# Splitting attention's queries and keys into rounded part and rest at the projection instead of at each head

## The chip, the cores and the metric

The kernel runs on one core of one Trainium2 chip. The metric is the device time of one execution in microseconds; the time before is the median of three runs. The engines are named as in the profile: PE is TensorE's matrix multiplication and PEld its loading of weights, DVE is VectorE, ACT is ScalarE, POOL is GpSimd, SP is SyncE, which here only issues transfers. ACT and POOL issue transfers too.

## What is computed

One layer of a hybrid encoder, for a prompt of 2048 rows of 1024 and for eight short samples of 16 rows each, with shared weights, all in fp32:

```
h = RMSNorm(x);  z = h @ w_in          # q, k, v of attention; q, k, v, o and gates of an mLSTM
A = chunk-band attention               # 8 heads x 64, chunks of 64, own chunk and 8 before it
B = mLSTM matrix memory                # 4 heads x 128, blocks of 64 in the reference
x = x + RMSNorm(concat(RMSNorm_A(A), sigmoid(o) * headRMSNorm_B(B)) @ w_out)
x = x + RMSNorm(ConvFFN(RMSNorm(x)))   # up, causal depthwise conv, gated GELU, down; D_FF = 2816
```

The outputs are the new x of both groups, the last 512 keys and values of the prompt, the samples' keys and values, and the mLSTM and convolution states.

## The kernel before, in words

Matrix products are done in three passes at fp32r, TensorE's rounded form of fp32: each operand is split into a rounded part (hi) and the rest (lo = value minus hi), and `mm3` (L93 to L97) adds hi x hi, hi x lo and lo x hi. ACT makes hi by a copy into an fp32r tile, DVE makes lo by a subtraction.

**Stage 1, the projection** (`hymba_step`, the loop over `seq`): the prompt's rows are done in two halves, 14 groups of weight columns in each. Groups `qk0` to `qk3` give attention's queries and keys, two heads each, transposed (columns on partitions, rows on the free axis), by `group_T`: six accumulators a group, three for the queries and three for the keys, each of 384 rows (256 for the last of the second half), each of 24 matmuls into one of the two PSUM banks of the tag `mm`. When an accumulator is done, ACT copies it to a tile `qk_st` in SBUF (`evac_scaled`, L224 and L226; the queries are scaled there), and `store_T` (L239) issues the stores to DRAM tensors `qTd`, `kTd` of one pair of heads and 512 rows each, from ACT's queue; the last 512 rows and the samples' rows also go to the outputs. `qk_st` has two buffers.

**Attention** is worked in beside the projection. `load_head` takes a head and a segment of 512 rows. First it fetches the 64 partitions of its queries twice (L334), onto partitions 0 to 63 and 64 to 127 of a raw tile, and those of its one or two segments of keys twice also (L337). Then ACT rounds the queries (L342) and DVE turns the upper half into the rest (L343), and for each segment of keys ACT makes `kh` (L346) and DVE `kl` (L347); values are fetched into raw tiles (L351) and split later (L355, L356). So the queries' two parts lie on the two halves of the partitions, and `att_unit` gets the scores of 128 rows from two matmuls (L382, L383), one with `kh` and one with `kl`, each summing over hi and lo of the queries. Then come bias and minimum on DVE (L393), exp on ACT (L394), PE transposes (`pt`), the split of the weights (L405 on ACT, L406 on DVE) and the product with the values (`ot`, L418, L419). The raw tiles have three buffers, `kh`, `kl` and `qs` two each.

**What sets the order.** `pump` is a planner: the projection yields declared costs (PE, DVE) after every 12 matmuls, and `pump` steps two pipes, attention and mLSTM, in turn while the declared DVE time is below `SHARE` times the declared PE time, at most two steps a call. `load_head` declares 0.6 + 0.6 for each segment of keys for its splits. Afterwards the framework orders each engine's instructions, and the issues of transfers, by its own estimate of when they become ready; on the chip each queue runs in that order.

**Stage 2**, `project`: the product with w_out, 17 tiles of 128 rows, with what is left of attention and the mLSTM worked in until tile 8. For tiles 0 to 7 the turned rows pass through the `mm` banks, which the product uses too, for later ones through the `big` banks (L67, L198, L199). **Stage 3** is the feed-forward part, more than half of the span, in three blocks of rows.

The samples' keys are split in `keys` inside `attention_sample`, in the same `kh` and `kl` tiles; this work stays.

Of the kernel before, what the change touches and what calls it, by code (L numbers as in the profile page):

```python
# [10 lines left out]
F32 = mybir.dt.float32  # L11
F32R = mybir.dt.float32r
# [5 lines left out]
P = 128  # L18
# [26 lines left out]
def hymba_step(ctx: ExitStack, tc: tile.TileContext, I: dict, O: dict):  # L45
# [14 lines left out]
    def ps_sm(name):  # L60
        return psum.tile([P, 512], F32, tag="sm", name=name)

    def dt_(shape, name):
        return dram.tile(shape, F32, tag=name, name=name)

    def transpose(out, in_, n=P):
        nc.tensor.transpose(out, in_, ident[:n, :n])  # L67
# [31 lines left out]

    kTs = dt_([P, 4, 128], "kTs")  # L100
    vs = dt_([P, 512], "vs")
    kTd = [[dt_([P, 512], f"kTd{p}_{s}") for s in range(4)] + [kTs[:, p, :]] for p in range(4)]
    qTd = [[dt_([P, 512 if s < 4 else 128], f"qTd{p}_{s}") for s in range(5)] for p in range(4)]
    vd = [[dt_([P, 4, 256], f"vd{p}_{s}") for s in range(4)] + [vs[:, p * 256:(p + 1) * 256].unsqueeze(1)]
          for p in range(2)]
    qkbd = [[dt_([P, 2, 512 if s < 4 else 128], f"qkbd{p}_{s}") for s in range(5)] for p in range(4)]
# [56 lines left out]
        return iter([])  # L163

    EARLY = 2
    SHARE = 0.615
    clock = [0.0, 0.0]
    turn = [0]
    pipes = []
# [69 lines left out]
                nc.scalar.dma_start(d[:, off:off + n * P], stage[:, j * P:(j + n) * P])  # L239
            j += n  # L240

    def group_T(wh, wl, half, chunks, dsts, scales, name, outs=(None, None)):
        for c in range(2):
            for ci, tiles in enumerate(HALVES[half]):
                n = len(tiles) * P
                ch = chunks[ci]
                acc = ps_mm(f"{name}_{c}_{ci}")
                for k in range(KT):
                    w = slice(k * 256 + c * P, k * 256 + (c + 1) * P)
                    mm3(acc[:, :n], wh[:, w], wl[:, w], ch[:, 0, k, :n], ch[:, 1, k, :n],  # L250
                        start=(k == 0), stop=(k == KT - 1))
                    if k % 4 == 3:
                        yield n * 12 / 2400, 0.0
                stage = pa.tile([P, 384], F32, tag="st", name=f"{name}_st{c}_{ci}", bufs=2)
                evac_scaled(stage[:, :n], acc[:, :n], scales[c])
                store_T(stage, dsts[c], tiles, outs[c])
# [64 lines left out]
    def load_head(s):  # L321
        pair, kg, hh, h, nm = s.pair, s.kg, s.hh, s.h, s.nm
        if kg % 2 == 0:
            nb = pa.tile([P, 640], F32, tag="nb", name=f"nb{nm}", bufs=2)
            nc.sync.dma_start(nb, bias_src(h, P, 640))
            nc.gpsimd.memset(nb[0:64, 576:640], BIG)
            nc.gpsimd.memset(nb[64:128, 0:64], BIG)
            nbs[hh] = nb
        s.nb = nbs[hh]
        rows = slice(hh * 64, hh * 64 + 64)  # L330
        qr = raw_tile(f"qraw{nm}")[:, :512]
        krs = [raw_tile(f"kraw{nm}_{g}")[:, :512] for g in s.segs]
        for r in range(2):
            nc.sync.dma_start(qr[r * 64:r * 64 + 64, :], qTd[pair][kg][rows, :])  # L334
        for kr, g in zip(krs, s.segs):
            for r in range(2):
                nc.sync.dma_start(kr[r * 64:r * 64 + 64, :], kTd[pair][g][rows, :])  # L337
        yield 0.0, 0.0
        s.kh = pa.tile([P, 1024], F32R, tag="kh", name=f"kh{nm}", bufs=2)
        s.kl = pa.tile([P, 1024], F32R, tag="kl", name=f"kl{nm}", bufs=2)  # L340
        s.qs = pa.tile([P, 512], F32R, tag="qs", name=f"qs{nm}", bufs=2)
        nc.scalar.copy(s.qs, qr)  # L342
        nc.vector.tensor_tensor(s.qs[64:128], qr[64:128], s.qs[64:128], op=ALU.subtract)  # L343
        for si, kr in enumerate(krs):
            c = slice(si * 512, (si + 1) * 512)
            nc.scalar.copy(s.kh[:, c], kr)  # L346
            nc.vector.tensor_tensor(s.kl[:, c], kr, s.kh[:, c], op=ALU.subtract)  # L347
        new = [g for g in s.segs if g == kg or (h, g) not in vhl]
        vrs = [raw_tile(f"vraw{nm}_{g}")[:, :4 * DA].rearrange("p (a d) -> p a d", a=4) for g in new]
        for vr, g in zip(vrs, new):  # L350
            nc.sync.dma_start(vr, vd[h // 4][g][:, :, (h % 4) * DA:(h % 4 + 1) * DA])  # L351
        yield 0.0, 0.6 + 0.6 * len(krs)
        for vr, g in zip(vrs, new):
            t = pa.tile([P, 4, P], F32R, tag="vhl", name=f"vhl{nm}_{g}", bufs=4)
            nc.scalar.copy(t[:, :, 0:DA], vr)  # L355
            nc.vector.tensor_tensor(t[:, :, DA:P], vr, t[:, :, 0:DA], op=ALU.subtract)  # L356
            vhl[h, g] = t
        s.v = {g: vhl[h, g] for g in s.segs}
        if kg % 2:
            for g in s.segs:  # L360
                vhl.pop((h, g))
        yield 0.0, 0.34 * len(new)
# [456 lines left out]
    def attention_sample(b0, b1):  # L819
# [22 lines left out]
        def keys(b, p_):  # L842
            if p_ == 0 and (b % 4 == 0 or b == b0):
                s.own = pa.tile([P, 4, 64], F32, tag="sh", name=f"own{b}", bufs=1)
                nc.sync.dma_start(s.own, kTs[:, :, b // 4 * 64:b // 4 * 64 + 64])
            kr = raw_tile(f"skr{b}_{p_}")
            nc.sync.dma_start(kr[:, 0:512], I["cache_k"][b, p_])
            nc.gpsimd.tensor_copy(kr[:, 512:LS], s.own[:, p_, b % 4 * DS:b % 4 * DS + DS])
            yield 0.0, 0.0
            kh = pa.tile([P, 1024], F32R, tag="kh", name=f"skh{b}_{p_}", bufs=2)[:, :LS]  # L850
            kl = pa.tile([P, 1024], F32R, tag="kl", name=f"skl{b}_{p_}", bufs=2)[:, :LS]
# [349 lines left out]
    for n_, (half, gi) in enumerate(seq):  # L1201
# [10 lines left out]
                            [O["v_prompt"][i], O["v_sample"][i].unsqueeze(1)])  # L1212
        elif g[:2] == "qk":
            it = group_T(wh, wl, half, chunks, [qTd[i], kTd[i]], [-(DA ** -0.5), None], nm,
                         [None, [O["k_prompt"][i], O["k_sample"][i]]])
# [479 lines left out]
```

## Time and profile before

| what | value |
|---|---|
| median of 3 runs | 2788.76 us (2788.08 to 2790.21) |
| profiled execution, first to last instruction | 2784.7 us |
| instructions | 47088 |
| bytes moved by DMA | 486.05 MB, 175 GB/s in the mean |
| mean granted clock of TensorE | 0.998 |

The profile is of one execution. Its span, 2784.7 us, lies 4.06 us under the median of the runs; a time worked out from the span is carried over to the runs by adding these 4.06 us, since the profiled execution's own time from end to end is not among the numbers. A row of the view by windows gives, for a stretch of time, its length, each engine's busy time with the number of its instructions, the granted clock, and the DMA engines' share and rate. A row of waits gives the engine and line that waited, who released it, the sum in us, the number of waits and the longest. A row of a timeline gives start, duration (us), engine, line, operation, and in brackets how long the engine had been idle and who ended it.

### The profile page before, as it was taken

To read this page: it belongs to the slowest core of one execution; us is meant where nothing else is said; L and a number is where in the kernel's file an instruction comes from. 1 tells how busy PE (TensorE), PEld (TensorE's weight loads), DVE (VectorE), ACT (ScalarE), POOL (GpSimd) and SP (SyncE) were. 2 spreads that over 40 slices of the span, in tenths; PEclk is the share of its full clock that TensorE was granted. 3 is DMA by queue.
4 is the path that set the end of the run, shared out by engine and by line. 5 is a ranking of instruction groups with operands and counts; after the bars stand their busy time and mean duration, and the time that the engine had idled before them with its cause. 6 is when DMAs were issued, how large, how long until landed. Compare 5 with 4: busy or idle time off the path is not lost.

```text
span 2784.7 us, 47088 instructions
## 1 busy us (share of the span) xinstructions
PE 2723.8 (98%) x16587; PEld 2548.3 (92%) x16587; DVE 1876.3 (67%) x3447; ACT 1409.1 (51%) x2836; POOL 437.4 (16%) x895
## 2 busy tenths in 40 slices
PE   8999999999999999999999999999999999999998
PEld 7899999998899998888999988899999878999887
DVE  5344455656556668666999986457877864888855
ACT  4355555644356666544454555345455543555543
POOL 1000010212000003244111110011111310222220
PEclk9999999999999999999999999999999999999999
DMA  5544355557555555356655455644544774555585
GB/s 185 155 119 136 103 174 162 164 157 217 162 173 148 144 179 171 107 176 227 187 172 167 167 176 174 219 142 153 160 152 141 276 263 152 172 179 180 192 309 190
DMA packets 311883, 486.05 MB, mean 175 GB/s; under 512 B 55426, under 2 KB 150622, under 8 KB 311518
## 3 DMA queue, kind: packets, MB, share of 16 engines
q1 hardware_dynamic: 271134, 442.92, 50.1%
q10 hardware_dynamic: 38592, 33.83, 3.6%
q0 software_dynamic: 1920, 6.29, 0.6%
q8 instruction: 130, 2.13, 0.3%
q14 instruction: 107, 0.88, 0.1%
HBM read 359.36 MB, written 126.70 MB: 175 GB/s over the span
## 4 chain that ended last, share of the span: by engine, by line
PE 55%; DVE 2%; DMA 1%; issue 1%; ACT 1%; POOL 1%; SPq 0%; DVEq 0%; POOLq 0%; ACTq 0%
PE uec L95 6%; PE uec L96 6%; PE uec L97 6%; PE dn L97 4%; PE dn L96 4%; PE dn L95 4%; PE ua L97 3%; PE ua L95 3%; PE ua L96 3%; PE dnm L97 2%; PE dnm L95 2%; PE dnm L96 2%; PE wo L97 2%; PE wo L95 2%; PE wo L96 2%; PE ub L96 1%
## 5 line engine op out<-in xcount | busy, mean ns | idle before, releaser
L95 PE MATMUL uec<-B,wuh 128*128 128x384 f32 (+1 forms) x720 | 234.9, 328 | 2.2 <-DVE uu L1419 1.1
L96 PE MATMUL uec<-B,wuh 128*128 128x384 f32 (+1 forms) x720 | 235.1, 327 | 0.0
L97 PE MATMUL uec<-B,wul 128*128 128x384 f32 (+1 forms) x720 | 233.9, 327 | 0.0
L1266 DVE TENSOR_TENSOR gl<-gr,gh 128x768 fp32r<-128x768 f32 (+3 forms) x141 | 120.4, 863 | 145.8 <-ACT gh L1265 144.5
L1265 ACT CAST gh<-gr 128x768 fp32r<-128x768 f32 (+3 forms) x141 | 102.0, 735 | 200.1 <-PE dn L96 183.2
L1265 ACT CAST wuh<-wu 128x512 fp32r<-128x512 f32 x255 | 141.7, 617 | 112.1 <-PE uec L96 103.2
L95 PE MATMUL dn<-wdh,gh 128*128 128x512 f32 x466 | 182.4, 391 | 2.3 <-DVE ug L1419 2.3
L96 PE MATMUL dn<-wdl,gh 128*128 128x512 f32 x466 | 183.4, 394 | 0.0
L97 PE MATMUL dn<-wdh,gl 128*128 128x512 f32 x466 | 167.9, 396 | 0.0
L1266 DVE TENSOR_TENSOR wul<-wu,wuh 128x512 fp32r<-128x512 f32 x255 | 164.6, 683 | 2.8 <-DMA x2d<-mx 2.8
L393 DVE CUSTOM_DVE_ANT_0 tmp<-s,nb 128x640 f32<-128x640 f32 (+4 forms) x128 | 94.4, 737 | 96.6 <-PE s L383 94.8
L95 PE MATMUL vo<-wi_h,hT 128*128 128x256 f32 x544 | 155.1, 285 | 0.6 <-DVE mt L199 0.6
L97 PE MATMUL vo<-wi_h,hT 128*128 128x256 f32 x544 | 155.6, 286 | 0.0
L96 PE MATMUL vo<-wi_l,hT 128*128 128x256 f32 x544 | 154.8, 285 | 0.0
L95 PEld LDWEIGHTS uec<-B,wuh 128*128 128x128 f32 x720 | 135.0, 188 | 4.2 <-DVE uu L1419 1.6
L95 PE MATMUL qk<-hT,wi_h 128*128 128x384 f32 (+1 forms) x384 | 128.7, 335 | 7.4 <-ACT qk_st L224 6.6
L96 PEld LDWEIGHTS uec<-B,wuh 128*128 128x128 f32 x720 | 135.2, 188 | 0.2
L97 PEld LDWEIGHTS uec<-B,wul 128*128 128x128 f32 x720 | 135.1, 188 | 0.0
L406 DVE TENSOR_TENSOR ptl<-pt,pth 128x640 fp32r<-128x640 f32 (+4 forms) x128 | 93.6, 737 | 57.1 <-ACT pth L405 56.0
L394 ACT ACTIVATE tmp<-tmp,mn 128x640 f32<-128x640 f32 (+4 forms) x128 | 97.6, 762 | 64.6 <-DVE mn L393 61.9
L96 PE MATMUL qb<-hT,wi_h 128*128 128x384 f32 (+1 forms) x384 | 127.8, 333 | 0.0
L96 PE MATMUL qk<-hT,wi_h 128*128 128x384 f32 (+1 forms) x384 | 127.6, 332 | 0.0
(412 smaller groups left out, 8873.0 us busy)
## 6 DMA issues: line engine op xcount, KB each, us to landing
wu<-in_w_up SPq DMA_DIRECT2D x220, 256.0 KB, 4.1
wu<-wsd SPq DMA_DIRECT2D x176, 256.0 KB, 4.2
wdr<-in_w_down SPq DMA_DIRECT2D x132, 256.0 KB, 5.6
gr<-gd SPq DMA_DIRECT2D x78, 384.0 KB, 3.6
wi_raw<-in_w_in SPq DMA_DIRECT2D x52, 512.0 KB, 4.0
wsd<-ws SPq DMA_DIRECT2D x88, 256.0 KB, 2.8
gd<-g SPq DMA_DIRECT2D x44, 384.0 KB, 3.5
kraw<-kTd SPq DMA_DIRECT2D x112, 128.0 KB, 3.2
```

What stands on the lines that cost most here:

```text
L95: nc.tensor.matmul(out, ah, bh, start=start, stop=False, skip_group_check=onto)
L96: nc.tensor.matmul(out, ah, bl, start=False, stop=False, skip_group_check=onto)
L97: nc.tensor.matmul(out, al, bh, start=False, stop=stop, skip_group_check=onto)
L393: nc.vector.tensor_tensor_reduce(o_, s_, b_, 1.0, 3e38, ALU.add, ALU.min, accum_out=mn)
L394: nc.scalar.activation(tmp[:, :n], tmp[:, :n], AF.Exp, bias=mn, scale=-1.0, accum_out=rsum[:, i % 4, hh:hh + 1])
L406: nc.vector.tensor_tensor(s.ptl[:, sl, qc], ptv, s.pth[:, sl, qc], op=ALU.subtract)
L1265: nc.scalar.copy(h, r)
L1266: nc.vector.tensor_tensor(l, r, h, op=ALU.subtract)
```

## The change

The split moves from the head to the projection. `group_T` gets a flag `parts`, set for the qk groups. With it, a new helper `store_parts` writes hi and lo side by side into one tile of two parts (`sthl`, three buffers), hi by ACT and lo by DVE, both straight from PSUM, and stores both with one transfer to `qTd`, `kTd`, which have now room for both parts. Where the accumulator holds rows that also go to an output (or are a sample's), it is first copied to a tile of SBUF as before, and hi and lo are made from there. `load_head` then fetches the queries' hi onto the lower and lo onto the upper half of the partitions, and both parts of the keys twice, straight into the tiles that PE reads. Its casts and subtractions go. `kh` and `kl` become one tile `khl` of the same size with two buffers. The planner gets other numbers: 0.28 of DVE for every 12 matmuls of a qk group, nothing for `load_head`'s second part, and `SHARE` 0.59 for 0.615. The reserve in SBUF for descriptors of POOL's transfers is set to 4096 bytes per partition.

```diff
-    SHARE = 0.615
+    SHARE = 0.59
...
+    def store_parts(acc, scale, dst, tiles, out, name):
+
+        n = len([t for t in tiles if t != SAMPLE]) * P
+        hl = pa.tile([P, 2, 384], F32R, tag="sthl", name=f"{name}_hl", bufs=3)
+        hi, lo = hl[:, 0, :n], hl[:, 1, :n]
+        src = acc[:, :n]
+        tail = [] if out is None else [t for t in tiles if 12 <= t < SAMPLE]
+        if SAMPLE in tiles or tail:
+            stage = pa.tile([P, 384], F32, tag="st", name=f"{name}_st", bufs=2)
+            evac_scaled(stage[:, :len(tiles) * P], acc[:, :len(tiles) * P], scale)
...
+            src, scale = stage[:, :n], None
+        evac_scaled(hi, src, scale)
+        if scale is None:
+            nc.vector.tensor_tensor(lo, src, hi, op=ALU.subtract)
+        else:
+            nc.vector.scalar_tensor_tensor(lo, src, scale, hi, op0=ALU.mult, op1=ALU.subtract)
+        j = 0
+        while j * P < n:
+            t = tiles[j]
+            m = min(4 - t % 4, n // P - j)
+            nc.scalar.dma_start(dst[t // 4][:, :, t % 4 * P:(t % 4 + m) * P], hl.bitcast(F32)[:, :, j * P:(j + m) * P])
+            j += m
...
                     if k % 4 == 3:
-                        yield n * 12 / 2400, 0.0
+                        yield n * 12 / 2400, 0.28 if parts else 0.0
+                if parts:
+                    store_parts(acc, scales[c], dsts[c], tiles, outs[c], f"{name}_{c}_{ci}")
+                    continue
...
-        qr = raw_tile(f"qraw{nm}")[:, :512]
-        krs = [raw_tile(f"kraw{nm}_{g}")[:, :512] for g in s.segs]
+        khl = pa.tile([P, 2, 1024], F32R, tag="khl", name=f"khl{nm}", bufs=2)
+        s.kh, s.kl = khl[:, 0, :], khl[:, 1, :]
+        s.qs = pa.tile([P, 512], F32R, tag="qs", name=f"qs{nm}", bufs=2)
         for r in range(2):
-            nc.sync.dma_start(qr[r * 64:r * 64 + 64, :], qTd[pair][kg][rows, :])
-        for kr, g in zip(krs, s.segs):
-            for r in range(2):
-                nc.sync.dma_start(kr[r * 64:r * 64 + 64, :], kTd[pair][g][rows, :])
+            at = slice(r * 64, r * 64 + 64)
+            nc.sync.dma_start(s.qs.bitcast(F32)[at, :], qTd[pair][kg][rows, r, :])
+            for si, g in enumerate(s.segs):
+                nc.sync.dma_start(khl.bitcast(F32)[at, :, si * 512:(si + 1) * 512], kTd[pair][g][rows, :, :])
         yield 0.0, 0.0
-        nc.scalar.copy(s.qs, qr)
-        nc.vector.tensor_tensor(s.qs[64:128], qr[64:128], s.qs[64:128], op=ALU.subtract)
-        for si, kr in enumerate(krs):
-            c = slice(si * 512, (si + 1) * 512)
-            nc.scalar.copy(s.kh[:, c], kr)
-            nc.vector.tensor_tensor(s.kl[:, c], kr, s.kh[:, c], op=ALU.subtract)
...
-        yield 0.0, 0.6 + 0.6 * len(krs)
+        yield 0.0, 0.0
...
-    nc = bacc.Bacc("TRN2", target_bir_lowering=False, num_devices=1)
+    nc = bacc.Bacc("TRN2", target_bir_lowering=False, num_devices=1, dynamic_dma_scratch_size=4096)
```

More of the change, by code (lines that the diff above doesn't have):

```diff
@@ L61, in ps_sm, with dt_ @@
         return psum.tile([P, 512], F32, tag="sm", name=name)
-    def dt_(shape, name):
-        return dram.tile(shape, F32, tag=name, name=name)
+    def dt_(shape, name, dtype=F32):
+        return dram.tile(shape, dtype, tag=name, name=name)
     def transpose(out, in_, n=P):
@@ L101, in hymba_step @@
     vs = dt_([P, 512], "vs")
-    kTd = [[dt_([P, 512], f"kTd{p}_{s}") for s in range(4)] + [kTs[:, p, :]] for p in range(4)]
-    qTd = [[dt_([P, 512 if s < 4 else 128], f"qTd{p}_{s}") for s in range(5)] for p in range(4)]
+    kTd = [[dt_([P, 2, 512], f"kTd{p}_{s}") for s in range(4)] + [kTs[:, p, :]] for p in range(4)]
+    qTd = [[dt_([P, 2, 512], f"qTd{p}_{s}") for s in range(4)] + [dt_([P, 128], f"qTd{p}_4")] for p in range(4)]
     vd = [[dt_([P, 4, 256], f"vd{p}_{s}") for s in range(4)] + [vs[:, p * 256:(p + 1) * 256].unsqueeze(1)]
@@ L240, in store_T, with group_T @@
             j += n
-    def group_T(wh, wl, half, chunks, dsts, scales, name, outs=(None, None)):
+    def store_parts(acc, scale, dst, tiles, out, name):
[7 more added lines that the diff above has]
+            evac_scaled(stage[:, :len(tiles) * P], acc[:, :len(tiles) * P], scale)
+            for j, t in enumerate(tiles):
+                c = slice(j * P, (j + 1) * P)
+                if t == SAMPLE:
+                    for d in [dst[4]] + ([] if out is None else [out[1]]):
+                        nc.scalar.dma_start(d, stage[:, c])
+            if tail:
+                m = len(tail) * P
+                nc.scalar.dma_start(out[0][:, tail[0] % 4 * P:tail[0] % 4 * P + m], stage[:, n - m:n])
+            src, scale = stage[:, :n], None
[10 more added lines that the diff above has]
+            j += m
+    def group_T(wh, wl, half, chunks, dsts, scales, name, outs=(None, None), parts=False):
         for c in range(2):
@@ L849, in keys @@
             yield 0.0, 0.0
-            kh = pa.tile([P, 1024], F32R, tag="kh", name=f"skh{b}_{p_}", bufs=2)[:, :LS]
-            kl = pa.tile([P, 1024], F32R, tag="kl", name=f"skl{b}_{p_}", bufs=2)[:, :LS]
+            khl = pa.tile([P, 2, 1024], F32R, tag="khl", name=f"skhl{b}_{p_}", bufs=2)
+            kh, kl = khl[:, 0, :LS], khl[:, 1, :LS]
             nc.scalar.copy(kh, kr)
@@ L1214, in hymba_step @@
             it = group_T(wh, wl, half, chunks, [qTd[i], kTd[i]], [-(DA ** -0.5), None], nm,
-                         [None, [O["k_prompt"][i], O["k_sample"][i]]])
+                         [None, [O["k_prompt"][i], O["k_sample"][i]]], True)
         elif g[:2] == "qb":
```

3 lines of the change are left out of this document (removed).

## The prediction

> **What bounds the kernel now.** I read the page first, then the view by windows cut at the stages, then the waits of PE, then the timeline at the longest of them.
>
> ```profile
> span 2784.7 us, 47088 instructions
> ...
> PE 2723.8 (98%) x16587; PEld 2548.3 (92%) x16587; DVE 1876.3 (67%) x3447; ACT 1409.1 (51%) x2836; POOL 437.4 (16%) x895
> ```
>
> ```profile
> core 0: us, PE busy (x) PEld busy (x) DVE busy (x) ACT busy (x) POOL busy (x), PEclk, DMA share, GB/s
> 48.00:115.00 67.00, 59.58 (x337) 56.84 (x338) 21.75 (x84) 17.24 (x42) 1.35 (x6) 0.97 0.56 160
> 115.00:557.00 442.00, 438.49 (x3218) 431.89 (x3218) 234.09 (x538) 235.70 (x557) 32.54 (x94) 1.00 0.47 143
> 557.00:736.00 179.00, 170.53 (x1140) 159.05 (x1140) 99.52 (x307) 75.66 (x203) 31.11 (x96) 1.00 0.58 177
> 736.00:1045.00 309.00, 305.50 (x2330) 300.85 (x2331) 187.84 (x427) 187.79 (x448) 19.89 (x60) 1.00 0.55 164
> 1045.00:1200.00 155.00, 151.65 (x884) 130.43 (x883) 114.55 (x224) 86.02 (x220) 45.90 (x68) 1.00 0.43 135
> 1200.00:1310.00 110.00, 108.36 (x522) 87.86 (x522) 75.66 (x73) 45.64 (x95) 52.50 (x65) 1.00 0.59 199
> 1310.00:2785.00 1475.00, 1454.64 (x7900) 1347.88 (x7898) 1114.52 (x1751) 734.27 (x1230) 244.08 (x475) 1.00 0.57 188
> ```
>
> PE bounds it: 2784.7 - 2723.8 = 60.9 us idle in all. The change takes no matmul away and adds none, so it can only win idle time of PE, or lose more of it. Idle time in the stages that it touches is length minus busy: 7.4 (the first two qk groups), 3.5, 8.5 (the second half's qk groups), 3.5, 3.4 and 1.6 us, 27.9 together. The feed-forward part, with 20.4 us, runs the same instructions before and after. So nothing above about 28 us can be won, whatever ACT and DVE save. What PE waits for in the first stages:
>
> ```profile
> PE qk L95 <- ACT qk_st L224: 6.6, 2, 3.3
> PE cus L781 <- DMA cs<-in_state_c: 5.0, 6, 2.0
> PE pt L67 <- DVE ptl L406: 1.8, 1, 1.8
> ```
>
> The largest row is two waits for the eviction of a qk accumulator, both before 115 us. The timelines of ACT, PE and PEld there:
>
> ```profile
> 81.98 0.62 ACT L342 CAST qs<-qraw 128x512 fp32r<-128x512 f32 x1 [10.99 <-DMA qraw<-qTd]
> 82.50 0.47 ACT L224 COPY qk_st<-qk 128x384 f32<-128x384 f32 x1
> ...
> 108.02 0.48 ACT L224 COPY qk_st<-qk 128x384 f32<-128x384 f32 x1 [7.30 <-DMA qTd<-qk_st]
> ...
> 83.03 0.45 PE L95 MATMUL qk<-hT,wi_h 128*128 128x384 f32 x1 [3.24 <-ACT qk_st L224]
> ...
> 104.70 0.33 PE L96 MATMUL qk<-hT,wi_h 128*128 128x384 f32 x1
> 104.87 0.34 PE L97 MATMUL qk<-hT,wi_l 128*128 128x384 f32 x1
> 108.55 0.69 PE L95 MATMUL qk<-hT,wi_h 128*128 128x384 f32 x1 [3.34 <-ACT qk_st L224]
> ...
> 108.72 0.33 PEld L96 LDWEIGHTS qk<-hT,wi_h 128*128 128x128 f32 x1
> ...
> 111.60 0.33 PEld L96 LDWEIGHTS qk<-hT,wi_h 128*128 128x128 f32 x1
> 111.92 0.20 PEld L97 LDWEIGHTS qk<-hT,wi_l 128*128 128x128 f32 x1
> ```
>
> In the first, ACT stood 10.99 us at a head's query cast, whose transfer had not landed; the finished accumulator's eviction was queued behind it, PE had no bank and stood 3.24 us. In the second, ACT stood 7.30 us because both `qk_st` buffers still waited for their stores, and PE stood 3.34 us. After that PE ran slow: weight loads start 0.32 us apart from 108.72 to 111.92 (ten steps), where matmuls of the same shape started 0.17 apart before (104.70, 104.87). That is 10 x 0.15 = 1.5 us more, and the granted clock of that window is 0.97.
>
> The Trainium skill, "TensorE: Matmul & The Clock Gate", in "What's actually happening", says that an idle window of about 3.4 us halves TensorE's clock and that the window runs free of the program. The trace agrees so far: of two gaps of nearly one length only one was followed by slow matmuls, for about 3.2 us. By that rule a stall of this length costs up to half as much again, and removing it wins that too; by the waits alone the sum below would lose its term of 1.5.
>
> **The change part by part.**
>
> Casts and subtractions of the heads go:
>
> ```profile
> L342 ACT CAST qs<-qraw x32: 606/617/640, 82.0 to 1118.9; 128x512 fp32r<-128x512 f32 x32
> L343 DVE TENSOR_TENSOR qs<-qraw,qs x32: 689/690/777, 82.6 to 1120.5; 64x512 fp32r<-64x512 f32 x32
> ...
> L346 ACT CAST kh<-kraw x56: 605/620/642, 88.2 to 1118.4; 128x512 fp32r<-128x512 f32 x56
> L347 DVE TENSOR_TENSOR kl<-kraw,kh x56: 678/685/889, 88.8 to 1119.7; 128x512 fp32r<-128x512 f32 x56
> ...
> L226 ACT ACTIVATE qk_st<-qk x24: 378/486/497, 55.7 to 730.6; 128x384 f32<-128x384 f32 x20, 128x256 f32<-128x256 f32 x4
> L224 ACT COPY qk_st<-qk x24: 360/472/480, 70.5 to 747.9; 128x384 f32<-128x384 f32 x20, 128x256 f32<-128x256 f32 x4
> ```
>
> ACT loses 32 x 0.617 + 56 x 0.620 = 54.5 us, DVE 32 x 0.690 + 56 x 0.685 = 60.4. ACT keeps 48 evictions (now hi) and gains 16 casts from SBUF for the accumulators with samples or kept keys; between a 0.36 and a 0.62 row I take 0.45, 7 us. DVE gains 48 subtractions, 40 of them of 384 columns or fewer out of PSUM. The nearest row is a PSUM subtraction's twin, an addition of that shape:
>
> ```profile
> L1493 DVE TENSOR_TENSOR x<-x,uec 128x384 f32<-128x384 f32 x44 | 24.2, 549 | 11.3 <-PE uec L97 11.2
> ```
>
> 48 x 0.549 = 26.4 us. Net: ACT -47, DVE -34 us. Beside a PE that is busy 98% this is worth nothing by itself: cost 0, with the matmuls as cover. What counts is where the two stood in PE's way.
>
> **Stall 1 goes**: ACT no longer waits for a query transfer ahead of an eviction. **Stall 2 goes**: stores now have three buffers, so an eviction waits for the third store back; accumulators come 24 x 0.17 = 4.1 us apart, so a store has 12 us where it had 8, and the wait was 7.3 us with about 3.3 too late. With the slow matmuls: 3.24 + 3.34 + 1.5 = 8.1 us won, at least 0 (if another wait on ACT takes their place, as that of the value split L355, which stays).
>
> **A new wait on banks**: a bank is free only after ACT's hi and DVE's lo, 0.49 + 0.55 = 1.04 us instead of 0.49, plus whatever holds DVE. The other bank's accumulator takes 4.1 us, so 3.1 us of lateness on DVE are free. Queued behind are the stores (on ACT, which now stands until lo is made) and, behind them on ACT, exps and casts of attention and of the next weights. DVE's waits:
>
> ```profile
> DVE tmp L393 <- PE s L383: 94.8, 52, 13.2
> ```
>
> Mean 1.8 us, so the typical one fits. The cost lies between 0 and both stalls over again; in the first groups, where the two evictions above ran late, less is free, so I take 1.0 us, nearest to the mean wait less what ACT's own lateness gives back.
>
> **Transfers.** As many issues as before on SP (64 + 112) and on ACT, but keys move both parts:
>
> ```profile
> kraw<-kTd SPq DMA_DIRECT2D x112, 128.0 KB, 3.2
> ...
> mqk<-qkbd SPq DMA_DIRECT2D x32, 256.0 KB, 3.4
> ...
> svr<-in_cache_v SPq DMA_DIRECT2D x32, 256.0 KB, 4.5
> ```
>
> That is 112 x 128 KB = 14.7 MB more fetched and 2 x 2048 x 512 x 4 B = 8.4 MB more stored, 5% of 486 MB, in a stage whose DMA share is about 0.5. A load takes 3.4 to 4.5 instead of 3.2 us and is asked for one whole head ahead: cost 0, covered by four attention units. The loads now wait on SP for PE to finish the scores of the head two before (`khl`, `qs` have two buffers); queued behind are weight and mLSTM loads. In return the value loads lose their wait for `kl` (a raw buffer):
>
> ```profile
> SPq L351 <- DVE kl L347: 49.4, 16, 8.5
> ```
>
> Bounds: -5.0 (the state loads of the `cus` row, which queue behind them; counted below) to +5.0 (as much again); 0, since no wait of PE above names the loads that queue there now. POOL's smaller reserve touches 24 transfers of the last blocks, issued by an engine 16% busy: 0, or some us if a full reserve holds the small copies behind them.
>
> **The planner.** In a qk group 12 matmuls of 384 declare 1.92, which allowed 0.615 x 1.92 = 1.18 of other work and now allow 0.59 x 1.92 - 0.28 = 0.85, 28% less. So the mLSTM sample batches (`cus`), which wait for their state in those groups, come slower: of their 5.0 us I take 1.5 (0 to 5.0). Elsewhere a head of two segments declares about 8.5 before (1.8 + 0.34 for loads, 4 x 1.33 for scores, 1.0 for outputs) and 6.7 after, so attention runs (8.5 / 6.7) x (0.59 / 0.615) = 1.2 times as fast. Twenty score units come after 1045 us now (the view of the tile `s` from there on):
>
> ```profile
> L393 DVE CUSTOM_DVE_ANT_0 tmp<-s,nb x20: 806/816/825, 1045.9 to 1176.4; 128x640 f32<-128x640 f32 x20
> ```
>
> Forty-four of the second half's 64 units come before 1045, so 1.2 times as many leave about ten or fewer. They are moved to 736 to 1045 us, where PE idled 3.5 of 309 us. What they leave is w_out with less cover: tiles 1 to 7 turn their rows through the banks of the product. Uncovered, each would cost PE (rows of the chain and of the lines) an eviction (DVE copy), the square and cast on ACT and the subtraction, less the transposes:
>
> ```profile
> 1163.83 0.73 ACT mt L1016 x2
> ...
> L1014 DVE COPY mx<-wo x34: 676/681/694, 1056.7 to 1314.6; 128x512 f32<-128x512 f32 x34
> ...
> L198 ACT CAST mt<-mT_pt x25: 564/592/1018, 1039.8 to 1299.9; 128x512 fp32r<-128x512 f32 x16, 128x1024 fp32r<-128x1024 f32 x9
> ```
>
> 0.68 + 0.73 + 0.59 + 0.69 (as L347) - 0.9 = 1.8 us, 12.6 for seven tiles. Against it stand up to 3.4 us of idle time there that attention's own chain makes (L406 above). The later tiles, almost without attention, idle 1.6 in 110 us, no worse: I take 0, between -3.4 and +12.6.
>
> **Sum**: -8.1 + 1.0 - 1.5 + 0 = -8.6 on the span, 2776.1; plus the 4.06 between span and median, 2780.2 us.
>
> **The rivals.**
>
> 1. *The time stays.* ACT and DVE lose work that PE never waited for, and another wait on ACT (L355 for its values, the stores for lo) holds the same two evictions. For it: the value transfers held ACT in the same stretch; 60.9 idle us are mostly elsewhere. Against: the longest wait on ACT, 10.99 us, is removed outright. Time 2788, at most 5 us off.
>
> 2. *Slower: DVE gives the banks back late.* Place: the 48 evictions. It decides where DVE starts lo over 3.1 us after hi. DVE waits up to 13.2 us for scores that PE does in between; if two evictions in each half meet such a wait, four stalls of 3.3 + 0.75 stand where two stood: +8.1, 2797. Against: in the second half's qk groups DVE is busy 56% and attention's scores are absent.
>
> 3. *It gains more*: the `cus` waits (5.0) and attention's chain in w_out (3.4) go as well: -8.1 - 5.0 - 3.4 = -16.5, 2772. For it: both are late chains that slower pumping loosens.
>
> That the split saves nothing and the planner's numbers alone do the work is the part of 3 that a run with the old numbers would tell apart.
>
> **How the numbers follow.** The forecast, 2775 to 2783, has 0.47; rival 3 0.09; rival 1 0.26; rival 2 0.18. A measurement tells 0.2%, 5.6 us, from no change. Faster by more (under 2783.2): 0.47 + 0.09 = 0.56; within: 0.26; slower (over 2794.3): 0.18. Most of the chance, 0.82, lies with faster and no change; the likeliest case alone has 2775 to 2783. The range takes in rival 3 and the uncovered w_out tiles on top of the forecast (2780.2 + 12.6 = 2793): 2769 to 2793, leaving out most of rival 2.
>
> **What would show it.** Right: no wait of PE for a qk eviction near 80 or 105 us, PEclk 1.00 there; 48 new DVE subtractions of about 0.55; `s` hardly after 1060 us; the span from 1310 to the end unchanged. Wrong: rows of PE waiting for DVE's lo or for `khl`; w_out idle over 5 us; a feed-forward part longer than 1475 us, which I have no mechanism for beyond POOL's reserve.

## The result, and the profile after

The changed kernel takes 2837.01 us (median of 4 runs, 2833.34 to 2838.84); the kernel before, run beside it on the same chip, takes 2789.35 us. The ratio is 1.0168 with a 95% interval of 1.0154 to 1.0182: **slower by 1.7%**, where 2780.2 was forecast. The profiled execution has a span of 2837.1 us, 52.4 more than before. These are the rows of its page that answer to those of before:

```profile
span 2837.1 us, 46877 instructions
...
PE 2743.7 (97%) x16587; PEld 2563.4 (90%) x16587; DVE 1840.7 (65%) x3407; ACT 1372.2 (48%) x2764; POOL 432.5 (15%) x895
```

PE does the same 16587 matmuls. It is idle 93.4 us instead of 60.9 (+32.5) and busy 19.9 us longer, which makes the 52.4. The longer busy time is slow matmuls: the mean granted clock fell from 0.998 to 0.991, and 0.9% of 2837 us less 0.2% of 2785 us is the same 20 us. ACT and DVE did get their relief, 36.9 and 35.6 us, and it bought nothing.

Where the time went is read best from the view by windows, cut at the same points of the program: the end of the second query-key group, of the `qb2` group of the first half, of the last query-key group, the first matmul of w_out, the first of the feed-forward part, and the end. Columns are length, then busy time of PE, PEld, DVE, ACT and POOL, PEclk, DMA share and GB/s. First the kernel before:

```profile
0.00:114.50 114.50, 94.16 (x597) 89.89 (x598) 49.94 (x128) 43.50 (x84) 11.34 (x39) 0.99 0.58 177
114.50:401.50 287.00, 287.00 (x2050) 284.02 (x2049) 138.74 (x308) 147.61 (x341) 8.62 (x29) 1.00 0.43 128
401.50:746.60 345.10, 331.59 (x2376) 316.03 (x2375) 200.19 (x551) 169.18 (x432) 55.84 (x162) 1.00 0.58 174
746.60:1045.80 299.20, 297.23 (x2276) 293.05 (x2274) 183.53 (x416) 183.67 (x440) 19.07 (x58) 1.00 0.54 162
1045.80:1313.50 267.70, 262.71 (x1414) 220.30 (x1413) 191.36 (x300) 130.86 (x312) 99.01 (x133) 1.00 0.50 164
1313.50:2784.70 1471.20, 1451.14 (x7885) 1345.07 (x7883) 1112.57 (x1748) 734.27 (x1230) 243.47 (x474) 1.00 0.57 188
```

And the kernel after, cut at the same six points:

```profile
0.00:112.10 112.10, 94.86 (x600) 90.73 (x601) 53.87 (x139) 44.70 (x88) 12.41 (x40) 0.98 0.64 203
112.10:402.70 290.60, 289.70 (x2070) 286.43 (x2069) 130.00 (x302) 136.60 (x325) 6.62 (x29) 1.00 0.56 156
402.70:765.70 363.00, 335.70 (x2337) 320.41 (x2336) 196.94 (x542) 162.92 (x415) 53.03 (x162) 0.97 0.58 173
765.70:1072.40 306.70, 297.63 (x2248) 291.50 (x2247) 153.76 (x360) 160.66 (x382) 14.91 (x51) 0.99 0.65 175
1072.40:1368.10 295.70, 274.60 (x1457) 229.57 (x1457) 191.50 (x319) 132.99 (x327) 100.08 (x140) 0.98 0.51 162
1368.10:2837.10 1469.00, 1451.25 (x7885) 1344.75 (x7883) 1114.61 (x1749) 734.29 (x1230) 245.48 (x474) 1.00 0.57 188
```

The stages differ by -2.4, +3.6, +17.9, +7.5, +28.0 and -2.2 us. The first query-key groups won, as meant. The loss lies after 400 us, most of it in w_out, whose own instructions nobody edited. Length less PE busy is the idle time: of the 34.8 us of new idle time before the feed-forward part, 13.8 lie in the third stage, 7.1 in the fourth and 16.1 in w_out (-3.1 and +0.9 in the first two). PE's waits are no single row but many; these five are longer than in before or new:

```profile
PE mT_pt L67 <- DVE mr L1011: 10.7, 5, 5.3
PE cus L807 <- DMA cs<-in_state_c: 9.1, 3, 5.5
PE ma L724 <- DVE num L730: 4.9, 3, 2.5
PE spt L67 <- ACT stmp L906: 4.1, 2, 3.3
PE sot L97 <- DVE spl L917: 4.0, 2, 2.5
```

None of these tiles (w_out's rows, the mLSTM state, the mLSTM and sample attention chains) is touched by the split. The longest wait of the `cus` row, from the timelines of PE and ACT, and the wait of SP for which the state load stood (the view of waits, 540 to 556 us):

```profile
543.58 0.61 PE L807 MATMUL cus<-cs,qz 128*128 128x129 f32 x4
...
553.00 1.20 PE L807 MATMUL cus<-cs,qz 128*128 128x129 f32 x4 [5.48 <-DMA cs<-in_state_c]
...
556.58 0.41 PE L96 MATMUL va<-wi_l,hT 128*128 128x264 f32 x1
556.80 0.32 PE L97 MATMUL va<-wi_h,hT 128*128 128x264 f32 x1
556.96 0.28 PE L95 MATMUL va<-wi_h,hT 128*128 128x264 f32 x1
```

```profile
SPq L795 <- DMA mixd<-num: 5.2, 1, 5.2
```

The load queue stood 5.2 us at the state load (the profile puts it to an mLSTM store), so the transfer landed late and PE stood 5.48 us. Then the clock: the same four matmuls take 1.20 us where they took 0.61, and steps of 0.22 us go back to 0.12 only at 556.96, 4.0 us on. And the longest wait in w_out, ACT ahead of PE:

```profile
1122.67 0.42 ACT L674 ACTIVATE mvo<-mvo 128x256 f32<-128x256 f32 x1 [4.70 <-DMA mvo<-vobd]
1123.11 0.37 ACT L717 ACTIVATE kw<-ms,colsp 128x128 f32<-128x128 f32 x1
1123.38 0.62 ACT L1042 ACTIVATE mt<-mx 128x512 fp32r<-128x512 f32 x1
1123.90 0.19 ACT L1042 ACTIVATION_READ_ACCUMULATOR mt<-mx 128x1 f32 x1
1124.12 0.63 ACT L1009 ACTIVATE mt<-mr 128x512 fp32r<-128x512 f32 x1
```

```profile
1129.72 1.97 PE L67 MATMUL mT_pt<-ident,mr 128*128 128x128 f32 x8 [5.31 <-DVE mr L1011]
```

ACT stood 4.70 us for an mLSTM value transfer (L674). Behind it in ACT's queue stood the square of w_out's next row (L1009); POOL's root, DVE's scaling and PE's transposes followed from it, and PE stood 5.31 us. In both cases the wait starts with the place that an instruction has in an in-order queue. In the second, the scaling's own 2.56 us (L1011, last section) are nearly half of it, a cost that before has too.

### The profile page after: what moved, and what is told of

Same layout as the page of the kernel before. It is cut to its first block, busy times and chain, and to the rows that moved or that the text cites. A ratio compares the mean times of both kernels' runs of the same rounds, so it can differ in the third digit from the quotient of the medians.

```text
span 2837.1 us, 46877 instructions
## 1 busy us (share of the span) xinstructions
PE 2743.7 (97%) x16587; PEld 2563.4 (90%) x16587; DVE 1840.7 (65%) x3407; ACT 1372.2 (48%) x2764; POOL 432.5 (15%) x895
## 4 chain that ended last, share of the span: by engine, by line
PE 51%; DVE 2%; DMA 1%; issue 1%; ACT 0%; POOL 0%; SPq 0%; DVEq 0%; POOLq 0%; ACTq 0%
PE uec L95 6%; PE uec L96 6%; PE uec L97 6%; PE dn L97 4%; PE dn L96 4%; PE dn L95 4%; PE ua L97 3%; PE ua L96 3%; PE ua L95 3%; PE dnm L97 2%; PE dnm L95 2%; PE dnm L96 2%; PE ub L96 1%; PE ub L97 1%; PE ub L95 1%; PE wo L95 1%
## 5 line engine op out<-in xcount | busy, mean ns | idle before, releaser
L97 PE MATMUL qk<-hT,wi_l 128*128 128x384 f32 (+1 forms) x384 | 129.0, 336 | 0.0
```

The source lines that it names most:

```text
L97: nc.tensor.matmul(out, al, bh, start=False, stop=stop, skip_group_check=onto)
```

## The experiments

Times of kernels sent together are compared with runs of the kernel before on the same chip, which gave medians of 2791 to 2795 us. "Before" and "after" are the two kernels of this case.

### Which part of the edit: reserve, planner's numbers, bytes

**e1**, only the reserve, in before:

```diff
-    nc = bacc.Bacc("TRN2", target_bir_lowering=False, num_devices=1)
+    nc = bacc.Bacc("TRN2", target_bir_lowering=False, num_devices=1, dynamic_dma_scratch_size=4096)
```

> The kernel before with one edit, the descriptor reserve set to 4096 as in the kernel after. If the reserve makes the loss, about 2837 us. By all the other theories (planner numbers, doubled key transfers, new order) the reserve does nothing: 2783 to 2795 us.

Measured 2793.58 us, ratio 1.0001 (0.9991 to 1.0010). The reserve costs nothing.

**e2**, only the planner's numbers, in before:

```diff
-    SHARE = 0.615
+    SHARE = 0.59
-                        yield n * 12 / 2400, 0.0
+                        yield n * 12 / 2400, 0.28 if name[:2] == "qk" else 0.0
-        yield 0.0, 0.6 + 0.6 * len(krs)
+        yield 0.0, 0.0
```

> The kernel before with the changed kernel's three planner numbers (share 0.59, 0.28 reserved in each step of the qk groups, 0 declared for a head's loads) and nothing else. If the planner's numbers make the loss, 2825 to 2845 us. If the doubled key transfers make it, 2775 to 2795 us, since none are doubled here. If any new order of the work would cost as much, something between 2800 and 2850 us, with the loss in other places than in the kernel after.

Measured 2836.8 us, ratio 1.0157 (1.0140 to 1.0174). Three numbers, without one instruction of the split, make a loss of the same size as the whole change.

**e3**, the reverse: after with the planner's numbers of before.

```diff
-    SHARE = 0.59
+    SHARE = 0.615
-                        yield n * 12 / 2400, 0.28 if parts else 0.0
+                        yield n * 12 / 2400, 0.0
-        yield 0.0, 0.0
+        yield 0.0, 0.6 + 0.6 * len(s.segs)
```

> The changed kernel with the three planner numbers of the kernel before (share 0.615, no reserve in the qk groups, 0.6 + 0.6 for each segment of a head). If the planner's numbers make the loss, about 2780 us (the old order with the two eviction stalls gone). If the transfers make it, about 2837 us as after. A time between says how much each has.

Measured 2825.7 us, ratio 1.0112 (1.0093 to 1.0131). The split without the numbers loses too. So neither edit is "the" cause: each alone costs 1.1 to 1.6%, both together 1.7%. Costs that don't add up speak for something that either edit sets off.

**e4**, after with as few key bytes as before:

```diff
-        s.kh, s.kl = khl[:, 0, :], khl[:, 1, :]
+        s.kh, s.kl = khl[:, 0, :], khl[:, 0, :]
-                nc.sync.dma_start(khl.bitcast(F32)[at, :, si * 512:(si + 1) * 512], kTd[pair][g][rows, :, :])
+                nc.sync.dma_start(khl.bitcast(F32)[at, 0, si * 512:(si + 1) * 512], kTd[pair][g][rows, 0, :])
```

> The changed kernel, but a head fetches only the keys' rounded part and uses it in place of the rest too, so that the key loads move 14.7 MB less, as many bytes as before; it leaves out the product with the keys' rest. Order, stores and planner are as after. If the doubled key loads make the loss, 2785 to 2800 us. If the planner's numbers or the order make it, 2830 to 2840 us.

Measured 2838.06 us, ratio 1.0158 (1.0136 to 1.0180). The doubled keys are not it. (The order is nearly but not wholly that of after: 94% of TensorE's steps agree, counted as in the next section.)

### The order held

What both edits share is that the framework orders the instructions anew. Matched in the traces (a step is an operation with its tiles and shape, equal neighbours taken as one), TensorE's order in after agrees with that in before in 67% of the steps, that of e2 in 68%, of e3 in 70%. In e1 it is the same step for step. The re-ordering can be switched off:

```diff
-    with tile.TileContext(nc, schedule_with_timeline_sim=True) as tc:
+    with tile.TileContext(nc, schedule_with_timeline_sim=False) as tc:
```

**e5** is before with that edit, **e6** is e3 with it, **e7** is after with it.

> The kernel before with the framework's own re-ordering switched off (the time simulation of its scheduler), so that each engine takes its work much as the program lists it. It is the base for the next two, which have it off as well. If the re-ordering places the work well, this is slower than before, 2790 to 2850 us; no theory rests on its own value.

> The changed kernel with the planner numbers of before and the re-ordering off: TensorE's order is that of the run e5 but for 15 places in 10955 runs of equal steps, so what is left between the two is the split itself with its stores, loads and waits. If the split costs time (waits of the loads for the scores two heads back, stores behind lo, doubled keys), 20 to 40 us more than e5. If the order made the loss, 0 to 10 us less than e5, as the sum of the prediction had it (8.6).

> The changed kernel with its own planner numbers and the re-ordering off. If the planner's numbers are bad whatever the re-ordering, 20 to 50 us more than e6. If it is only the luck of the order that the re-ordering finds, within 10 us of e6.

Measured: e5 2883.51 us (2881.98 to 2884.69; ratio to before 1.0333), e6 2878.41 (2874.73 to 2879.14; 1.0312), e7 2883.77 (2879.64 to 2886.72; 1.0329). TensorE's steps in e5 and e6 agree in 99.8%. With the order so held the split saves 5 us, in the range that was expected of it, and the 33 us that it lost in e3 are not there. The planner's numbers then cost 5 us (e7 against e6), not 30.

e7 also tells what became of a step of the prediction, that attention runs faster under the new numbers. Each instruction of DVE line 419 (393 in before) is one score unit; what comes after the first w_out matmul is counted (x) in these rows of e6, e7 and after:

```profile
L419 DVE CUSTOM_DVE_ANT_0 tmp<-s,nb x18: 810/816/825, 1084.7 to 1231.4; 128x640 f32<-128x640 f32 x18
```

```profile
L419 DVE CUSTOM_DVE_ANT_0 tmp<-s,nb x3: 814/815/816, 1109.9 to 1118.4; 128x640 f32<-128x640 f32 x3
```

```profile
L419 DVE CUSTOM_DVE_ANT_0 tmp<-s,nb x20: 807/819/826, 1072.7 to 1203.4; 128x640 f32<-128x640 f32 x20
```

As listed, the new numbers leave 3 units instead of 18. As re-ordered, after leaves 20, as many as before left. What the planner lists is not what runs.

**e15** and **e16** repeat e5 and e6 with the share at 0.605 (between the two, TensorE's orders differ in 8 places):

```diff
-    SHARE = 0.615
+    SHARE = 0.605
```

> The kernel before with the re-ordering off and the share at 0.605: the base of the next run in a second order. If the order alone moves the time, another 10 us or more away from the run e5 (2883.5).

> The changed kernel with the planner numbers of before but the share at 0.605 and the re-ordering off; TensorE's order agrees with the run e15 but for 8 places. If the split by itself saves what the prediction said, 3 to 10 us less than e15. If the split itself costs time, 10 to 30 us more.

Measured 2889.8 us (2881.67 to 2894.72; 1.0343) and 2894.59 (2891.28 to 2895.29; 1.0355). Both expectations miss: the base moved 6 us and not 10, and the split costs 5 us here where it saved 5. The saving of the first pair is clear of the spread of its runs; the cost of the second is not, since e15 alone spreads over 13 us. In both a cost of 30 us is excluded. The saving of 8.6 us is excluded by the second pair only, and both pairs stand on an order that is 3% slower than that of before, so what the split is worth in before's own order was not measured.

### Other orders of the old code and of the new

If a new draw of the order costs, it must cost without any part of the change. **e8** and **e9** nudge before's share (0.605 and 0.63; counted as above, TensorE's order agrees in 89% and 92% of the steps), **e10** and **e11** do the same to e3, **e12** sets after's share to 0.61. All of them are the edit

```diff
-    SHARE = 0.615
+    SHARE = 0.605
```

with the values named (e12 goes from 0.59 to 0.61).

> The kernel before with its share nudged from 0.615 to 0.605 and nothing else; TensorE's order agrees with that of before in 92% of its steps. If the time hangs on the exact order (before stands on a tuned point), 10 to 40 us more than before. If only the larger moves of the changed kernel's numbers cost, within 6 us of before.

> The kernel before with its share at 0.63 in place of 0.615 (TensorE's order agrees in 91% of its steps). If before stands on a tuned point of the order, a nudge to this side costs as the one to 0.605 did: 2805 to 2835 us. If only less side work costs, within 6 us of before or below it.

> The changed kernel with the planner numbers of before, but the share at 0.605. If the loss is the luck of the order, the runs of the changed code scatter over the same 2785 to 2840 us as those of the old code, and this one lands anywhere there; if the split itself makes the loss under the re-ordering, it stays at 2815 to 2835 us as the run e3 did, whatever the share.

> The changed kernel with the planner numbers of before, but the share at 0.63. Luck of the order: anywhere from 2785 to 2840 us. The split itself: 2815 to 2835 us.

> The changed kernel with its own numbers, but the share at 0.61 in place of 0.59. If the lower share starves the side work and w_out pays for it, 2800 to 2825 us with the first step of the feed-forward part back before 1350 us. If it is the luck of the order, anywhere from 2785 to 2840 us.

Measured: e8 2816.88 us, ratio 1.0097 (1.0075 to 1.0119). e9 2815.55, 1.0076 (1.0061 to 1.0091). e10 2848.23, 1.0195 (1.0180 to 1.0210). e11 2832.04, 1.0142 (1.0125 to 1.0158). e12 2845.72, 1.0183 (1.0163 to 1.0203), the first feed-forward matmul at 1369.3 us, so a higher share does not free w_out. The old code loses 0.8 to 1.0% on either side of its value; it stands on a lucky or a tuned point. The new code scatters too, 1.1 to 2.0%, but at each share it lies above the old code, by 1.1, 1.0 and 0.7%.

**e13** and **e14** (share 0.605) undo the heads' half of the split in e3 and e10:

```diff
+        for r in range(2):
+            nc.sync.dma_start(qr[r * 64:r * 64 + 64, :], qTd[pair][kg][rows, 0, :])
...
+                nc.sync.dma_start(kr[r * 64:r * 64 + 64, :], kTd[pair][g][rows, 0, :])
...
-            nc.sync.dma_start(s.qs.bitcast(F32)[at, :], qTd[pair][kg][rows, r, :])
...
-                nc.sync.dma_start(khl.bitcast(F32)[at, :, si * 512:(si + 1) * 512], kTd[pair][g][rows, :, :])
...
+        nc.scalar.copy(s.qs, qr)
+        nc.vector.tensor_tensor(s.qs[64:128], qr[64:128], s.qs[64:128], op=ALU.subtract)
```

> The changed kernel with the planner numbers of before and the heads' part undone: the projection stores both parts, and a head fetches the rounded part as its raw data and splits it again as before (it leaves out the rests of queries and keys). It has the loads' bytes, casts and waits of before in the heads. If the heads' new loads and waits make what the split costs under the re-ordering, 2785 to 2805 us; if the projection's stores make it, 2820 to 2830 us; if the re-ordering is luck, anywhere from 2785 to 2850 us.

> The same at a share of 0.605. If the heads' part makes the cost, near the run e8 of the old code at this share, 2810 to 2825 us; if the projection's part makes it, near the run e10 of the changed code, 2840 to 2850 us; if the re-ordering is luck, anywhere from 2785 to 2850 us, and not on the same side as e13.

Measured 2829.19 us, 1.0121 (1.0108 to 1.0135), and 2831.64, 1.0138 (1.0122 to 1.0153): at 0.615 as much as the whole split; at 0.605 the step up from the old code (e8) is 0.4%, where the whole split's is 1.0%. The projection's half alone draws a new order and loses. One effect of the heads' half does show, in the fourth stage (last query-key group to w_out); the windows of e3, e4 and e13:

```profile
763.00:1075.20 312.20, 300.79 (x2285) 294.48 (x2284) 159.04 (x380) 164.43 (x404) 19.20 (x59) 1.00 0.66 179
```

```profile
756.80:1067.20 310.40, 299.06 (x2244) 291.96 (x2242) 153.68 (x360) 160.82 (x380) 15.23 (x51) 0.99 0.52 153
```

```profile
767.50:1064.60 297.10, 293.52 (x2221) 287.96 (x2220) 172.46 (x392) 174.20 (x415) 15.22 (x51) 0.99 0.53 157
```

PE idles 11.4 us there in e3, 11.3 in e4 with half the key bytes, 3.6 in e13. Over all runs with the re-ordering on, the six with the new heads idle 8.6 to 12.4 us in this stage, the six with the old heads in another order (e2, e8, e9, e13, e14 and e18 below) 3.4 to 6.7. So under the re-ordering the heads' new form goes with about 5 us, and the bytes are not its reason. With the order held the cost is not there: PE idles 8.6 us in this stage in e5 and in e6 (11.1 in e15, 13.1 in e16). Whether the loads' wait for the scores two heads back makes it, or the orders that the new loads draw, was not tried.

### An edit that can only help

**e17** gives the tiles of evicted accumulators a third buffer, in before (with e1's reserve, which makes room); the same edit stands at a second place, where a value accumulator is evicted. Every engine's order stays that of before.

```diff
-                stage = pa.tile([P, 384], F32, tag="st", name=f"{name}_st{c}_{ci}", bufs=2)
+                stage = pa.tile([P, 384], F32, tag="st", name=f"{name}_st{c}_{ci}", bufs=3)
```

> The kernel before with a third buffer for the tiles that hold an evicted accumulator until its store has landed (and the smaller reserve that makes room). Every engine's order is that of before, so this is the part of the change that ends the second eviction stall, with the order held. The stall's price in the prediction was 3.34 us and 1.5 us of slow matmuls: 4 to 5 us less than before if that stands, nothing if another wait on ScalarE takes its place.

**e18** gives the raw loads a fourth buffer, in before (with e1's reserve). It can only take waits away; counted as above, TensorE's order agrees with before in 73% of its steps.

```diff
-        return pa.tile([P, LS], F32, tag="raw", name=name, bufs=3)
+        return pa.tile([P, LS], F32, tag="raw", name=name, bufs=4)
```

> The kernel before with a fourth buffer for raw loads (and the same reserve): it takes waits off the load queue and adds no work, but the re-ordering gives it another order (82% of TensorE's steps agree). If the order's luck makes the time, 10 to 50 us more than before, although nothing in it can cost. If orders are alike and only work and waits count, 2780 to 2790 us.

e17: 2792.05 us, ratio 1.0005 (0.9994 to 1.0016). The second eviction stall is not cured, and its rows show why (timeline of ACT):

```profile
101.28 0.47 ACT L226 ACTIVATE qk_st<-qk 128x384 f32<-128x384 f32 x1
107.31 1.00 ACTq L239 DMA_DIRECT2D qTd<-qk_st  x2
108.35 0.48 ACT L224 COPY qk_st<-qk 128x384 f32<-128x384 f32 x1 [6.61 <-DMA qraw<-qTd]
```

The stores of the accumulator before this one (ACTq L239) were issued only at 107.31 us, 5.6 us after its eviction had ended, and the next eviction stood behind them in ACT's queue. In before it was the same:

```profile
106.86 0.89 ACTq L239 DMA_DIRECT2D qTd<-qk_st  x2
```

So ACT stood at the issue of these stores and not for a buffer, and a third buffer can't shorten that. The name in brackets is only that of the wait that ended last; e1, with two buffers and the same order, has the stores at 109.91 us and names the next head's query, 9.32 us. What the issue waited for stands in the traces' semaphores: in all three the one ahead of it was last released, just before the issue, by the landing of a weight load (`wi_raw`), in before at 106.78 us, 8.7 us after that load was issued. Stores and loads share these semaphores. That another wait on ACT holds the eviction is the first rival of the prediction, at its place.

e18: 2815.52 us, ratio 1.0084 (1.0071 to 1.0097). An edit that adds no work and removes waits costs 24 us. Half of its loss lies in w_out, as after's does (15.8 of 30.1 us in the traces, against 28.0 of 52.4); its third and fifth stage:

```profile
410.20:759.70 349.50, 329.26 (x2350) 314.25 (x2350) 193.03 (x540) 166.68 (x425) 50.65 (x162) 1.00 0.57 168
...
1061.90:1345.40 283.50, 272.00 (x1445) 227.01 (x1444) 194.61 (x315) 134.10 (x324) 101.11 (x138) 0.99 0.48 157
```

The third stage idles 20.2 us (13.5 in before, 27.3 in after), w_out 11.5 (5.0 and 21.1). Unlike after, e18 also loses 8.7 us in the first two stages (after: 1.2).

## Why the prediction was wrong, point by point

**The failed step** is the one under "The planner": from the declared costs it read how the work would lie ("attention runs 1.2 times as fast", "ten or fewer" units left, "what they leave is w_out with less cover: I take 0") and so took the planner's list for the order that runs. The sum let everything not edited keep its place. The framework orders the whole program anew after the planner, and the runs show what that costs: the two edits that left every engine's order as it was, e1 and e17, cost 0.0 and 0.05%; every edit that drew a new order from the re-ordering cost 0.8 to 2.0%, whether it was the split (e3), its projection half (e13), the planner's numbers (e2), a nudge of one of them (e8, e9) or a spare buffer (e18). With the order held the split costs or saves 5 us. That term, +23 to +44 us on the old code (e9 to e2), was missing from the sum, where it stood as w_out at 0 and as an unchanged place for everything not edited.

- **What bounds it.** Right that PE does, and that no more than 28 us of its idle time could be won. That bound is one of gain only; no bound stood on the other side, and idle time went from 60.9 to 93.4 us.
- **Casts and subtractions.** 48 DVE subtractions came (32 of them out of PSUM, not 40), the largest group at 0.554 us against 0.549 estimated; DVE lost 35.6 us (34), ACT 36.9 (47). Worth nothing, as said.

```profile
L265 DVE SCALAR_TENSOR_TENSOR qk_hl<-qk,qk_hl x20: 419/554/559, 58.1 to 748.3; 128x384 fp32r<-128x384 f32 x16, 128x256 fp32r<-128x256 f32 x4
...
  PEld qk L95: 0.8, 1
  PE qk L95: 0.5, 1
```

- **The two stalls** went: PE's only waits for the new eviction are the 0.8 and 0.5 us in the lower rows of that view ("who waited for it"). From the end of the first value group to that of the second query-key group after gained 7.1 us on before (it was 4.7 behind at 55 us and 2.4 ahead at 112), against 8.1 forecast. The number came, but not by the mechanism alone: e3, with the same split, stands 5.4 us for the eviction of a qk accumulator, longer than either stall of before (waits of PE, then the timeline of ACT):

```profile
PE qk L95 <- ACT qk_st L226: 5.4, 1, 5.4
```

```profile
107.92 0.69 ACT L715 ACTIVATE w<-mb,colsp 128x128 f32<-128x128 f32 x2 [9.95 <-POOL mb L699]
108.51 0.47 ACT L226 ACTIVATE qk_st<-qk 128x384 f32<-128x384 f32 x1
```

  There ACT stood 9.95 us at an mLSTM row ahead of the eviction. e10, e11 and e12, also with the split, stand 3.9, 3.7 and 3.0 us. So the split takes away the two reasons seen in before (the query cast outright), and the order decides whether another takes their place; that none did in after is luck of its order. The reading of the second stall was wrong as well: ACT stood at the issue of stores, not for the two buffers (e17). The sign "PEclk 1.00 there" came: the slow matmuls in after's first query-key groups lie before 56 us, ahead of both places.

```profile
48.00:56.00 8.00, 5.86 (x27) 5.63 (x28) 3.13 (x5) 2.11 (x4) 0.00 (x0) 0.79 0.38 95
56.00:115.00 59.00, 57.01 (x342) 54.57 (x341) 24.25 (x93) 18.36 (x45) 1.23 (x3) 1.00 0.60 183
```

- **Late banks** (rival 2, and +1.0 in the sum): not seen in after, by the 0.8 and 0.5 us above. e13 stands 8.1 us for a lo, but there DVE had itself waited 9.0 us for ACT's hi, which stood behind an mLSTM row. The sign "slower" came, the mechanism didn't.
- **Transfers at 0**: right for the bytes (e4). The 112 key loads land after 5.7 us at the median where 3.2 were before and I took at most 4.5:

```profile
khl<-kTd SPq DMA_DIRECT2D x112, 256.0 KB, 5.7
```

```profile
SPq L370 <- PE s L409: 52.8, 18, 10.5
```

  The new wait of the load queue for scores, in the row of SP's waits, is as long as the wait for `kl` that it replaced (49.4). Under the re-ordering the heads' form goes with about 5 us of idle time in the fourth stage that the sum did not have.
- **`cus`**: wrong in sign; 9.1 us instead of 5.0, with one wait of 5.48.
- **w_out at 0, up to +12.6**: 28.0 us, and the sign named for being wrong, over 5 us idle, came with 21.1. It is not for want of attention (20 units as before). More mLSTM is left in it, 16 units after w_out's start against 11 (instructions of `w` from there on, in after and in before), and in the stall at 1124 us a row of w_out stood behind one of them on ACT. But the count is not the reason by itself: e8 leaves 9 units and e10 10, and w_out idles 21.9 and 25.9 us there. The price of less cover shows in e7, as listed, where 3 score units are left: w_out idles 32.3 us against 28.3 in e6, 4 us more and inside the bounds.

```profile
L718 DVE TENSOR_TENSOR w<-ms,w x16: 277/282/293, 1087.5 to 1262.9; 128x128 f32<-128x128 f32 x16
```

```profile
L692 DVE TENSOR_TENSOR w<-ms,w x11: 277/284/292, 1049.8 to 1143.0; 128x128 f32<-128x128 f32 x11
```

- **The feed-forward part unchanged**: right, 1469.0 us against 1471.2.

The Trainium skill, "TensorE: Matmul & The Clock Gate", in "What's actually happening", has the clock come back after about 3.4 us of sustained work. The 4.0 us after the stall at 547 us agree. The idle window of about 3.4 us that the prediction drew on was not needed in full: a stall of 2.47 us was enough (last section).

**What stays open.** With the re-ordering on, the new code lies 0.7 to 1.1% above the old at equal shares; the 5 us of the heads (0.2%) are seen only there, and the rest may be the luck of few draws or come from how the new stores are ordered. What makes one order slower than another was followed for two waits of after only. And why the order of before is good was not found: three of its neighbours are 0.8 to 1.0% worse, so it may have been picked among many. No version that was run beats before.

## What to carry to other kernels

Where a framework re-orders the program by its own estimate, an edit has two prices: its own, and that of the new order, which in this kernel was a loss each time one was drawn. Compare the instruction orders first; if they differ, price the order by an edit that can do nothing (a spare buffer, a nudge of a number) on the old kernel, and the edit itself by a pair with the re-ordering off. A bound from idle time limits what can be won, not what can be lost.

## What the runs showed of the hardware

New idle time of PE brought slow matmuls with it, by each run's page against that of before: 19.9 us more busy time for 32.5 us more idle in after, 12.2 for 23.8 in e3, 11.3 for 18.8 in e18, 25.1 for 23.3 in e2. So each us of new idle time cost 1.5 to 2.1 us in all in these four. Most of the stalls were under 3 us long, and one of 2.47 us was enough for 3.4 us at half the clock, less than the 3.4 us of idle time that the prediction had reckoned with (timeline of PE, then the window, in after):

```profile
1007.82 0.80 PE L724 MATMUL ma<-cst,mqk 128*128 128x129 f32 x2 [2.47 <-DVE num L730]
```

```profile
1007.40:1010.80 3.40, 2.98 (x13) 2.98 (x14) 1.95 (x7) 3.18 (x10) 0.00 (x0) 0.50 0.29 90
```

The scaling of w_out's rows on DVE took from 0.48 to 2.62 us for one shape, in before and in after alike. In after the 13 of 17 that ran beside POOL's addition of 128x1024 took 2.56 to 2.62 us, the other four 0.48 to 0.51. In the stall at 1124 us it took 2.56, beside such an addition that ran from 1127.04 for 2.34 us:

```profile
1127.11 2.56 DVE L1011 TENSOR_SCALAR mr<-mr,att_rs 128x512 f32<-128x512 f32 x1 [0.71 <-POOL att_rs L84]
```
